# Sparse-attention outputs by tokens from unscaled weights, with a column of ones for the sums

## The chip, the cores and the metric

The kernel runs on one core of a Trainium2 chip. The metric is the device time of one launch, in microseconds (us). TensorE is PE in the profile (its weight loads are PEld), VectorE is DVE, ScalarE is ACT, GpSimd is POOL, and SyncE, which issues the large DMAs, is SP.

## The reference, cut to what matters

A two-layer transformer over 256 tokens of width 1024, in fp32. The first layer's mixer has 16 query heads of 64, in two groups that share keys and values, and three branches: compressed, selected and window. For each head the branch outputs are weighted by gates and added:

```python
s = jnp.where(mask, s, -inf)             # one branch, one head
e = jnp.exp(s - max(s))
p = e / sum(e)                            # masked_softmax
o = einsum('bthgk,bkgd->bthgd', p, v)     # p @ v, v: 64 wide, shared by 8 heads
out = g0 * o_cmp + g1 * o_slc + g2 * o_win
y = (out * sigmoid(z)) @ w_out
```

With 256 tokens the selected and the window branch both come down to causal attention here, each with its own keys and values, and both are computed in one loop.

## The kernel before, in words

`Net.run` calls the first layer's attention (`_nsa`), a dilated attention, feed-forward layers, a hybrid mixer and norms in turn. Weights come from DRAM in blocks of 128 x 2048 on SP's queue into the buffers `raw`; ACT makes a rounded high part (`hi`, L216), DVE the rest (`lo`, L219), and PE multiplies with both (banks `g`). Beside that, the modulation vectors of the layers are made on DVE from further blocks, two `scalar_tensor_tensor` of 128 x 1024 a block (L371). `self.step` and `self.fill` put such blocks, and matmuls of a projection that are ready early, between the steps of the attention. A scheduler at build time then sets a fixed order for each engine, and each engine runs its own in order.

PSUM has 8 banks: three with the tag `g`, two `s` (scores), two `t` (transposes), and **one** `o` (outputs). A bank is given to its next use when all readers of the last one are done.

The loop is `for j in range(8)`, one pair of heads (`hh` 0 and 1) per turn, numbered from pair 0; `g = j // 4` is the key group. For each head and each half of the query tokens (`q` = 1, tokens 128 to 255 against 256 keys; `q` = 0, tokens 0 to 127 against 128 keys) PE makes scores of both branches in a bank `s`, DVE takes their maxima (`mxs`, L925), ACT makes exponentials `p1` or `p0` (L927) and with `accum_out` their sums (`dens`). DVE inverts the sums (L929) and multiplies by the gates `gt` (L930); ACT scales `p1` (L934), DVE `p0` (L936). Three 128 x 128 transposes on PE (L213) bring each branch's weights into a bank `t` with the keys on the partitions, and a copy (L942, by ACT or DVE) puts them into one of six buffers (`kcat`, `kcp`, `pt0` to `pt2`, which hold 384 columns each).

The outputs come channels first. The values `vtok` (keys on the partitions, 64 channels) are the stationary operand, the weights of all 256 or the last 128 tokens are streamed, and the two heads write to the two halves of the partitions of one bank `o`, which also takes the compressed branch (`vb` stationary, `pct` streamed):

```python
ob = self.bank("o")
self.mm(ob[:, :256], vb[:, g, j % 4], pct[:, g], True, False)
...
va = vtok[:, k, br * 128 + g * 64:br * 128 + g * 64 + 64]
self.mm(ob[HALF[hh], 128 * k:256], va, pts[br, hh][:, 256 * k:256 + 128 * k], False, ...)
...
nc.scalar.copy(oT[:, j], ob[:, :256])    # L950
```

`oT` is then multiplied by the gate of `z` (L957), split into two parts, and goes into the output projection. L206 is the line of every matmul and L213 that of every transpose; an fp32 matmul appears as two passes.

Of the kernel before, what the change touches and what calls it, by code (L numbers as in the profile page):

```python
# [11 lines left out]
AF = mybir.ActivationFunctionType  # L12
ALU = mybir.AluOpType
# [5 lines left out]
HALF = slice(0, 64), slice(64, 128)  # L19
# [80 lines left out]
SC = ((0, 1), (1, 1))  # L100
# [57 lines left out]
class Net:  # L158
# [581 lines left out]
    def _nsa(self, xT):  # L740
        nc, A = self.nc, self.A
# [48 lines left out]
        i = nc.vector.tensor_tensor(self.og[:, :, 1], self.vec("final_g"), self.vec("final_g"), op=ALU.mult)  # L790
        self.tc.add_manual_dep(i.ins, self.applied.ins.name, NOSYNC, reason="norm first")
        nc.vector.tensor_scalar(self.og[:, :, 1], self.og[:, :, 1], EPS, None, op0=ALU.add)
        vtok = self.w([128, 512], tag="vtok", bufs=1).rearrange("p (q n) -> p q n", q=2)
        gt = self.w([128, 2, 16, 3], tag="gt", bufs=1)

        def ev_v(banks):
            for q in range(2):
                nc.vector.tensor_copy(vtok[:, q, :], banks[q][:, 0:256])
                nc.scalar.activation(gt[:, q].rearrange("p h r -> p (h r)"), banks[q][:, 256:304], AF.Tanh, scale=0.5)
            nc.vector.tensor_scalar(gt, gt, 1.0, None, op0=ALU.add)  # L800

        self.gemm(W, [(1408, 128), (1664, 128), (2816, 48)], act, ev_v, "B")
        zs = v8(self.b8())

# [13 lines left out]
        for vi, n in enumerate("kv"):  # L818
            ke = self.w([128, 16, 2, 16], tag="ke", bufs=1)
# [14 lines left out]
            t = self.t(self.sp, [32, 256], tag="hidt", bufs=1)  # L834
# [3 lines left out]
            b = self.bank("t")  # L838
# [7 lines left out]
        b = self.bank("t")  # L846
# [7 lines left out]
        vb = self.w([128, 2, 4, 128], tag="vb", bufs=1)  # L854
        bmv = self.C["bmv"].rearrange("p (j c) -> p j c", j=4)
        for g in range(2):
            b = self.bank("t")
# [19 lines left out]
        pc = self.w([128, 2, 16, 16], tag="pc", bufs=1)  # L877
        mx = self.w([128, 2, 16], tag="mx", bufs=1)
# [13 lines left out]
        pct = self.w([128, 2, 256], tag="pct", bufs=1)  # L892
        b = self.bank("t")
# [3 lines left out]
        nc.scalar.copy(pct.rearrange("p g t -> p (g t)"), b)  # L897

        kc, kp = self.w([128, 1024], tag="kcat", bufs=1), self.w([128, 512], tag="kcp", bufs=1)
        slots = [kc[:, :384], kc[:, 512:896], kp[:, :384]] + [self.t(self.sp, [128, 384], tag=f"pt{i}", bufs=1) for i in range(3)]  # L900
        self.rate = RN[1]
        oh, ol = (v8(self.b8(F32R)), v8(self.b8(F32R))) if OD[0] != (0, 1) or OD[1] != (0, 1) else (None, None)
        o32 = v8(self.b8()) if OD[0] or OD[1] else None
        oT = v8(self.b8())
        for j in range(8):
            g = j // 4
            self.fill(FN[6 + j])
            self.step(AN[6 + j])
            ob = self.bank("o")
            self.mm(ob[:, :256], vb[:, g, j % 4], pct[:, g], True, False)  # L910
            pts = {}
            for hh in range(2):
                h = 2 * j + hh
                p1 = self.t(self.sp, [128, 2, 256], tag="p1", bufs=2)
                p0 = self.t(self.sp, [128, 2, 128], tag="p0", bufs=2)
                mx = self.t(self.sp, [128, 2, 2], tag="mxs", bufs=2)
                den = self.t(self.sp, [128, 2, 2], tag="dens", bufs=2)
                for q in (1, 0):
                    p, nk = (p1, 256) if q else (p0, 128)
                    sb = self.bank("s")  # L920
                    sv = sb[:, :2 * nk].rearrange("p (b t) -> p b t", b=2)
                    for i, kx in enumerate((kh, kl)):
                        self.mm(sv, qs[g][:, j % 4, hh, q * 128:(q + 1) * 128], kx[:, g, :, :nk], i == 0, False)
                    self.mm(sv[:, :, nk - 128:], self.ibf, self.M["tri"][:, None, :].to_broadcast([128, 2, 128]), False, True)
                    nc.vector.tensor_reduce(mx[:, q], sv, axis=AX.X, op=ALU.max, negate=True)  # L925
                    for br in range(2):
                        nc.scalar.activation(p[:, br], sv[:, br], AF.Exp, bias=mx[:, q, br:br + 1],  # L927
                                             accum_out=den[:, q, br:br + 1])
                nc.vector.reciprocal(den, den)  # L929
                nc.vector.tensor_tensor(den, den, gt[:, :, h, 1:3], op=ALU.mult)  # L930
                for br in range(2):
                    for q, p in ((1, p1), (0, p0)):
                        if (br, q) in SC:
                            nc.scalar.activation(p[:, br], p[:, br], AF.Copy, scale=den[:, q, br:br + 1])  # L934
                        else:
                            nc.vector.tensor_scalar(p[:, br], p[:, br], den[:, q, br:br + 1], None, op0=ALU.mult)  # L936
                    tb = self.bank("t")
                    self.tr(tb[:, 0:128], p0[:, br, 0:128])
                    self.tr(tb[:, 128:256], p1[:, br, 0:128])
                    self.tr(tb[:, 256:384], p1[:, br, 128:256])  # L940
                    pt = slots[(4 * j + 2 * hh + br) % 6]
                    (nc.scalar.copy if (br, hh) in NPT else nc.vector.tensor_copy)(pt, tb[:, :384])  # L942
                    pts[br, hh] = pt

            for br in range(2):
                for k in range(2):
                    for hh in range(2):
                        va = vtok[:, k, br * 128 + g * 64:br * 128 + g * 64 + 64]
                        self.mm(ob[HALF[hh], 128 * k:256], va, pts[br, hh][:, 256 * k:256 + 128 * k], False, k == 1 and br == 1)
            nc.scalar.copy(oT[:, j], ob[:, :256])  # L950
        self.fill(99)
        for j in range(8):
            if o32 is None:
                t = self.w([128, 256], tag="xr", bufs=4)
            else:
                t = o32[:, j]
# [710 lines left out]
```

## Time and profile before

| | us |
|---|---|
| median of 3 runs (lowest, highest) | 1115.93 (1111.5, 1120.14) |
| the profiled execution | 1116.25 |
| its span in the trace | 1114.4 |
| PE busy in the span | 1059.9 |
| DVE busy | 859.6 |
| ACT busy | 615.9 |

The span runs from the first to the last instruction in the trace; the execution's own time is 1.85 us longer. The busy times are of the span. The mean granted clock of TensorE was 0.987 of full speed.

### The profile page before, as it was taken

The numbers are of one execution on the slowest core, as the hardware profiler recorded it, in microseconds if no ns is written. First come the engines' busy times: TensorE is split into PE (matmuls) and PEld (weight loads), VectorE is DVE, ScalarE is ACT, GpSimd is POOL, SyncE is SP. The second block draws the span as 40 slices with busy tenths as digits, with TensorE's granted clock in tenths as the row PEclk, the third lists the DMA queues.
The fourth block names the chain that finished last, engine by engine and source line by source line (L and its number), as shares of the span: only waits on it lengthen the run. The fifth ranks groups of instructions, "written<-read, shape, count | busy, mean of one in ns | idle before, by whom it ended". The sixth has DMA issues, their size and how long they took to land.

```text
span 1114.4 us, 20234 instructions
## 1 busy us (share of the span) xinstructions
PE 1059.9 (95%) x8145; PEld 990.3 (89%) x8145; DVE 859.6 (77%) x1571; ACT 615.9 (55%) x1190; POOL 64.3 (6%) x70
## 2 busy tenths in 40 slices
PE   5989999989999999999999899989999999999997
PEld 4958867877889899999989789989999999999997
DVE  7995987899999998888698789468866767555543
ACT  3482776788665544544378257525644556444442
POOL 0020000122000000000000030001000000000000
PEclk9898999999999999999999899999999999999998
DMA  8865466466868577887743433263436445554551
GB/s 332 336 223 189 155 224 232 174 242 226 310 238 296 177 291 302 299 300 282 288 153 128 142 114 114 83 187 114 149 121 246 169 158 181 189 190 170 173 186 39
DMA packets 33423, 226.34 MB, mean 203 GB/s; under 512 B 3681, under 2 KB 3937, under 8 KB 7346
## 3 DMA queue, kind: packets, MB, share of 16 engines
q1 hardware_dynamic: 32914, 224.20, 55.7%
q8 instruction: 64, 1.05, 0.4%
q10 hardware_dynamic: 288, 0.52, 0.1%
q0 software_dynamic: 128, 0.33, 0.1%
q14 instruction: 29, 0.24, 0.1%
HBM read 223.73 MB, written 1.31 MB: 202 GB/s over the span
## 4 chain that ended last, share of the span: by engine, by line
issue 35%; PE 21%; DVE 6%; DMA 2%; ACT 2%; POOL 1%; SPq 0%; POOLq 0%; DVEq 0%; ACTq 0%
PE g L206 14%; PE s L206 5%; DMA b<-dr 2%; DVE lo L219 1%; PE t L206 1%; PE o L206 1%; DVE w L1221 1%; PE t L213 1%; POOL rrq L1282 0%; DVE xt L1371 0%; ACT hi L216 0%; DVE b L1450 0%; DVE b L1459 0%; DVE xs L1372 0%; DVE d L1443 0%
## 5 line engine op out<-in xcount | busy, mean ns | idle before, releaser
L206 PE MATMUL g<-b,hi 128*128 128x256 f32 (+2 forms) x3696 | 688.0, 286 | 9.8 <-ACT b L586 8.1
L206 PEld LDWEIGHTS g<-b,hi 128*128 128x128 f32 (+1 forms) x3696 | 578.2, 191 | 16.2 <-ACT b L586 9.8
L206 PE MATMUL g<-b,lo 128*128 128x256 f32 (+2 forms) x1848 | 518.6, 285 | 8.6 <-DVE lo L219 8.6
L216 ACT CAST hi<-raw 128x1024 fp32r<-128x1024 f32 (+2 forms) x302 | 280.0, 953 | 222.1 <-PE g L206 117.2
L219 DVE TENSOR_TENSOR lo<-raw,hi 128x1024 fp32r<-128x1024 f32 (+2 forms) x302 | 329.8, 1114 | 90.2 <-ACT hi L216 89.8
L206 PEld LDWEIGHTS g<-b,lo 128*128 128x128 f32 (+1 forms) x1848 | 347.9, 190 | 12.0 <-DVE lo L219 10.4
L371 DVE SCALAR_TENSOR_TENSOR raw<-raw,scrow 128x1024 f32<-128x1024 f32 x120 | 146.0, 1238 | 4.9 <-DMA raw<-in_ws_dram 4.8
L206 PE MATMUL s<-b,hi 128*128 128x256 f32 (+1 forms) x288 | 62.8, 284 | 2.2 <-ACT w L546 2.2
L206 PE MATMUL s<-b,b 128*128 128x128 f32 (+2 forms) x224 | 49.8, 344 | 3.6 <-DVE b L682 1.9
L206 PE MATMUL g<-b,raw 128*128 128x256 f32 x208 | 51.3, 381 | 0.0
L206 PEld LDWEIGHTS s<-b,hi 128*128 128x128 f32 x288 | 48.4, 189 | 2.4 <-ACT w L546 2.4
L1221 DVE SCALAR_TENSOR_TENSOR w<-pad,u,w 128x256 f32<-128x256 f32 x96 | 41.7, 481 | 2.5 <-ACT w L1216 2.4
L206 PEld LDWEIGHTS g<-b,raw 128*128 128x128 f32 x208 | 37.1, 190 | 4.7 <-ACT w L546 0.2
L206 PEld LDWEIGHTS s<-b,b 128*128 128x128 f32 x224 | 30.1, 191 | 11.4 <-issue 4.5
L206 PE MATMUL s<-b,lo 128*128 128x256 f32 (+1 forms) x144 | 39.7, 283 | 0.0
L206 PE MATMUL t<-b,hi 128*128 128x256 f32 x160 | 37.5, 281 | 0.0
L927 ACT ACTIVATE p<-s,mxs 128x256 f32<-128x256 f32 (+1 forms) x64 | 26.5, 420 | 13.8 <-DVE dens L930 6.2
L1132 DVE TENSOR_TENSOR w<-w,g 128x512 f32<-128x512 f32 (+1 forms) x21 | 14.2, 675 | 23.7 <-PE g L206 23.7
L488 POOL TENSOR_TENSOR rcol<-rcol,u 128x2 f32<-128x2 f32 x5 | 3.5, 703 | 487.3 <-ACT rcol L487 487.3
L206 PE MATMUL g<-hi,b 128*128 128x512 f32 (+1 forms) x96 | 28.3, 371 | 2.4 <-ACT hi L216 2.3
L1130 ACT ACTIVATE w<-g 128x512 f32<-128x512 f32 (+1 forms) x21 | 12.3, 586 | 32.0 <-PE g L206 32.0
L206 PEld LDWEIGHTS t<-b,hi 128*128 128x128 f32 x160 | 28.5, 188 | 0.0
(329 smaller groups left out, 1314.2 us busy)
## 6 DMA issues: line engine op xcount, KB each, us to landing
raw<-in_ws_dram SPq DMA_DIRECT2D x202, 1024.0 KB, 4.8
b<-dr SPq DMA_DIRECT2D x8, 512.0 KB
raw<-in_ws_dram SPq DMA_DIRECT2D x4, 512.0 KB, 3.7
raw<-in_ws_dram SPq DMA_DIRECT2D x2, 608.0 KB, 3.8
b<-in_xT_dram SPq DMA_DIRECT2D x1, 1024.0 KB
u<-in_consts_dram SPq DMA_DIRECT2D x2, 384.0 KB
u<-in_consts_dram SPq DMA_DIRECT2D x1, 527.0 KB
u<-in_consts_dram SPq DMA_DIRECT2D x2, 256.0 KB, 5.5
```

What stands on the lines that cost most here:

```text
L206: i = self.nc.tensor.matmul(out, lhsT=lhsT, rhs=rhs, start=start, stop=stop, skip_group_check=True)
L213: self.nc.tensor.transpose(out, in_, self.ident[:k, :k])
L216: i = self.nc.scalar.copy(hi, src)
L219: self.nc.vector.tensor_tensor(lo, src, hi, op=ALU.subtract)
L371: nc.vector.scalar_tensor_tensor(r, r, 1.0, sc, op0=ALU.mult, op1=ALU.mult, accum_out=mod[:, n:n + 1])
L488: nc.gpsimd.tensor_tensor(r, r, self.mhalf[:, 0:2], op=ALU.pow)
L927: nc.scalar.activation(p[:, br], sv[:, br], AF.Exp, bias=mx[:, q, br:br + 1], accum_out=den[:, q, br:br + 1])
L1130: nc.scalar.activation(t, gb, AF.Tanh, scale=0.5)
L1132: nc.vector.tensor_tensor(t, t, ub, op=ALU.mult)
L1221: nc.vector.scalar_tensor_tensor(dst, fl(pad[:, o:o + 256]), taps[i], dst, op0=ALU.mult, op1=ALU.add)
```

## The change

`vtok` becomes `vone`, which holds 65 columns per half, branch and group: 64 of values and one of ones, set once by POOL. `accum_out`, the inversion per head and the scaling of `p1` and `p0` leave the loop, so the transposes and the copies take unscaled exponentials. For each pair and each half `q` (1, then 0) one bank `o` takes the compressed branch (now `pct` stationary, 128 columns of `vb` streamed) and, beside it, 65 columns for each head and branch (the weights stationary, `vone` streamed), so the tokens lie on the partitions and column 64 holds the sums. DVE inverts these (L947), multiplies by the gates (L948), scales the four 64-column pieces (`obs`, in the buffer `ke`; L950), adds the compressed branch (L951) and adds the two branches (L952) into `on`, in the buffer `pc`. After both halves, two transposes bring `on` into a bank `t`, and ACT copies it to `oT`. Lines below the loop move: L957 is L963 there.

```diff
@@ -790,12 +790,13 @@
         i = nc.vector.tensor_tensor(self.og[:, :, 1], self.vec("final_g"), self.vec("final_g"), op=ALU.mult)
         self.tc.add_manual_dep(i.ins, self.applied.ins.name, NOSYNC, reason="norm first")
         nc.vector.tensor_scalar(self.og[:, :, 1], self.og[:, :, 1], EPS, None, op0=ALU.add)
-        vtok = self.w([128, 512], tag="vtok", bufs=1).rearrange("p (q n) -> p q n", q=2)
+        vone = self.w([128, 2, 4, 65], tag="vtok", bufs=1)
+        nc.gpsimd.memset(vone[:, :, :, 64:65], 1.0)
         gt = self.w([128, 2, 16, 3], tag="gt", bufs=1)
 
         def ev_v(banks):
             for q in range(2):
-                nc.vector.tensor_copy(vtok[:, q, :], banks[q][:, 0:256])
+                nc.vector.tensor_copy(vone[:, q, :, :64], banks[q][:, 0:256].rearrange("p (v e) -> p v e", v=4))
                 nc.scalar.activation(gt[:, q].rearrange("p h r -> p (h r)"), banks[q][:, 256:304], AF.Tanh, scale=0.5)
             nc.vector.tensor_scalar(gt, gt, 1.0, None, op0=ALU.add)
 
@@ -897,6 +898,8 @@
         nc.scalar.copy(pct.rearrange("p g t -> p (g t)"), b)
 
         kc, kp = self.w([128, 1024], tag="kcat", bufs=1), self.w([128, 512], tag="kcp", bufs=1)
+        obs = self.w([128, 2, 2, 2, 64], tag="ke", bufs=1)
+        ons = self.w([128, 2, 2, 128], tag="pc", bufs=1)
         slots = [kc[:, :384], kc[:, 512:896], kp[:, :384]] + [self.t(self.sp, [128, 384], tag=f"pt{i}", bufs=1) for i in range(3)]
         self.rate = RN[1]
         oh, ol = (v8(self.b8(F32R)), v8(self.b8(F32R))) if OD[0] != (0, 1) or OD[1] != (0, 1) else (None, None)
@@ -906,15 +909,11 @@
             g = j // 4
             self.fill(FN[6 + j])
             self.step(AN[6 + j])
-            ob = self.bank("o")
-            self.mm(ob[:, :256], vb[:, g, j % 4], pct[:, g], True, False)
             pts = {}
             for hh in range(2):
-                h = 2 * j + hh
                 p1 = self.t(self.sp, [128, 2, 256], tag="p1", bufs=2)
                 p0 = self.t(self.sp, [128, 2, 128], tag="p0", bufs=2)
                 mx = self.t(self.sp, [128, 2, 2], tag="mxs", bufs=2)
-                den = self.t(self.sp, [128, 2, 2], tag="dens", bufs=2)
                 for q in (1, 0):
                     p, nk = (p1, 256) if q else (p0, 128)
                     sb = self.bank("s")
@@ -924,16 +923,8 @@
                     self.mm(sv[:, :, nk - 128:], self.ibf, self.M["tri"][:, None, :].to_broadcast([128, 2, 128]), False, True)
                     nc.vector.tensor_reduce(mx[:, q], sv, axis=AX.X, op=ALU.max, negate=True)
                     for br in range(2):
-                        nc.scalar.activation(p[:, br], sv[:, br], AF.Exp, bias=mx[:, q, br:br + 1],
-                                             accum_out=den[:, q, br:br + 1])
-                nc.vector.reciprocal(den, den)
-                nc.vector.tensor_tensor(den, den, gt[:, :, h, 1:3], op=ALU.mult)
+                        nc.scalar.activation(p[:, br], sv[:, br], AF.Exp, bias=mx[:, q, br:br + 1])
                 for br in range(2):
-                    for q, p in ((1, p1), (0, p0)):
-                        if (br, q) in SC:
-                            nc.scalar.activation(p[:, br], p[:, br], AF.Copy, scale=den[:, q, br:br + 1])
-                        else:
-                            nc.vector.tensor_scalar(p[:, br], p[:, br], den[:, q, br:br + 1], None, op0=ALU.mult)
                     tb = self.bank("t")
                     self.tr(tb[:, 0:128], p0[:, br, 0:128])
                     self.tr(tb[:, 128:256], p1[:, br, 0:128])
@@ -941,13 +932,28 @@
                     pt = slots[(4 * j + 2 * hh + br) % 6]
                     (nc.scalar.copy if (br, hh) in NPT else nc.vector.tensor_copy)(pt, tb[:, :384])
                     pts[br, hh] = pt
-
-            for br in range(2):
-                for k in range(2):
-                    for hh in range(2):
-                        va = vtok[:, k, br * 128 + g * 64:br * 128 + g * 64 + 64]
-                        self.mm(ob[HALF[hh], 128 * k:256], va, pts[br, hh][:, 256 * k:256 + 128 * k], False, k == 1 and br == 1)
-            nc.scalar.copy(oT[:, j], ob[:, :256])
+            on = ons[:, j % 2]
+            for q in (1, 0):
+                ob = self.bank("o")
+                ov = ob[:, :260].rearrange("p (h b e) -> p h b e", h=2, b=2)
+                cb = ob[:, 260:388].rearrange("p (h e) -> p h e", h=2)
+                f = self.mm(ob[:, 260:388], pct[:, g, q * 128:(q + 1) * 128], vb[:, g, j % 4])
+                for hh in range(2):
+                    for br in range(2):
+                        for k in range(q + 1):
+                            c0 = 128 * (q + k)
+                            self.mm(ov[:, hh, br], pts[br, hh][:, c0:c0 + 128], vone[:, k, br * 2 + g], False, k == q, f)
+                r = self.t(self.sp, [128, 2, 2], tag="dens", bufs=2)
+                nc.vector.reciprocal(r, ov[:, :, :, 64])
+                nc.vector.tensor_tensor(r, r, gt[:, q, 2 * j:2 * j + 2, 1:3], op=ALU.mult)
+                t = obs[:, q]
+                nc.vector.tensor_tensor(t, ov[:, :, :, :64], r[:, :, :, None].to_broadcast([128, 2, 2, 64]), op=ALU.mult)
+                nc.vector.tensor_tensor(t[:, :, 0], t[:, :, 0], cb, op=ALU.add)
+                nc.vector.tensor_tensor(on[:, q].rearrange("p (h e) -> p h e", h=2), t[:, :, 0], t[:, :, 1], op=ALU.add)
+            tb = self.bank("t")
+            for q in range(2):
+                self.tr(tb[:, q * 128:(q + 1) * 128], on[:, q])
+            nc.scalar.copy(oT[:, j], tb[:, :256])
         self.fill(99)
         for j in range(8):
             if o32 is None:
```

The order on the engines changes with it. On PE between pairs, before (bank `o_207` is pair 1's output, `o_224` pair 2's, `s_237` and `s_238` are scores):

```order
L206 MATMUL o_207_1187<-pt2_168_1024,vtok_101_673 64x256 [waits Activation_49]
L206 MATMUL o_207_1187<-pt0_166_1022,vtok_101_673 64x128
L206 MATMUL o_207_1187<-pt2_168_1024,vtok_101_673 64x128
L206 MATMUL s_237_1306<-b8_23_127,b8_26_130 128x512 [waits PE_49,Activation_49]
L206 MATMUL s_237_1306<-b8_23_127,b8_26_130 128x512
L206 LDWEIGHTS u150_150_913
L206 MATMUL s_237_1306<-u149_149_911,u150_150_913 128x2x128
L206 MATMUL s_238_1313<-b8_23_127,b8_26_130 128x256 [waits Activation_49]
L206 MATMUL s_238_1313<-b8_23_127,b8_26_130 128x256
L206 MATMUL o_224_1266<-pct_162_1013,vb_141_892 128x256 [waits Activation_49]
```

And the changed order there (`o_210` is pair 1's half `q` = 0, `o_227` pair 2's half `q` = 1, `t_212` the transposes of `on`, which is named `pc_167`; `t_218` those of pair 2's weights):

```order
L206 MATMUL o_210_1188<-vb_141_893,pct_162_1014 128x128 [waits DVE_49]
L206 MATMUL o_210_1188<-vtok_101_673,pt1_169_1026 128x65
L206 MATMUL o_210_1188<-vtok_101_673,pt2_170_1027 128x65
L206 MATMUL o_210_1188<-vtok_101_673,kcat_164_1021 128x65 x2
L206 MATMUL o_227_1258<-vb_141_893,pct_162_1014 128x128 [waits DVE_49,PE_49]
L213 MATMUL t_212_1200<-u7_7_89,pc_167_1024 128x128 [waits DVE_49]
L213 MATMUL t_212_1200<-u7_7_89,pc_167_1024 128x128
L213 MATMUL t_218_1221<-u7_7_89,p0_214_1205 128x128
L213 MATMUL t_218_1221<-u7_7_89,p1_213_1204 128x128 x2
```

The scores now stand ahead of pair 1's last half, and the compressed matmul of pair 2 and the transposes of `on` follow that half with no other matmul between.

On DVE at that place, before (the step from one head's sums to its scaled weights in pair 2; L371 and L219 are work of other layers or the projection):

```order
L929 RECIPROCAL dens_228_1271<-dens_228_1271 128x4 [waits Activation_49]
L925 TENSOR_REDUCE mxs_235_1304<-s_237_1306 128x2 [waits PE_49]
L930 TENSOR_TENSOR dens_228_1271<-dens_228_1271,gt_102_674 128x4 [waits DVE_49]
L668 SCALAR_TENSOR_TENSOR b8_116_754<-w5_323_1786,g_310_1662 128x512 [waits Activation_49]
L936 TENSOR_SCALAR p0_226_1269<-p0_226_1269,dens_228_1271 128x128 [waits DVE_49]
L936 TENSOR_SCALAR p0_226_1269<-p0_226_1269,dens_228_1271 128x128
L925 TENSOR_REDUCE mxs_235_1304<-s_238_1313 128x2 [waits PE_49]
L957 SCALAR_TENSOR_TENSOR b8_171_1027<-b8_172_1028,b8_116_754 128x256
L942 COPY kcat_164_1020<-t_231_1290 128x384 [waits PE_49]
```

And the changed order (the five steps on pair 1's half `q` = 0, in `o_210`):

```order
L947 RECIPROCAL dens_211_1194<-o_210_1188 128x4 [waits PE_49]
L371 SCALAR_TENSOR_TENSOR raw_353_1960,u15_15_109<-raw_353_1960,scrow_9_94 128x1024
L948 TENSOR_TENSOR dens_211_1194<-dens_211_1194,gt_102_675 128x4 [waits DVE_49]
L371 SCALAR_TENSOR_TENSOR raw_357_1973,u15_15_109<-raw_357_1973,scrow_9_94 128x1024 [waits DMAHW7_49]
L950 TENSOR_TENSOR ke_166_1023<-o_210_1188,dens_211_1194 128x256 [waits DVE_49]
L371 SCALAR_TENSOR_TENSOR raw_357_1973,u15_15_109<-raw_357_1973,scrow_9_94 128x1024
L951 TENSOR_TENSOR ke_166_1023<-ke_166_1023,o_210_1188 128x2x64 [waits DVE_49]
L952 TENSOR_TENSOR pc_167_1024<-ke_166_1023 128x128 [waits DVE_49]
L963 SCALAR_TENSOR_TENSOR b8_173_1030<-b8_174_1031,b8_116_755 128x256 [waits Activation_49]
```

Three L371 stand between the five steps, of which the first and third read the bank, as does the fourth.

On PE at the last pair, before (`o_292` is pair 7's output; `t_350` belongs to the output projection):

```order
L206 MATMUL o_292_1582<-kcat_164_1020,vtok_101_673 64x256 [waits Activation_49]
L206 MATMUL o_292_1582<-pt1_167_1023,vtok_101_673 64x128
L206 MATMUL o_292_1582<-kcat_164_1020,vtok_101_673 64x128
L206 MATMUL o_292_1582<-pt2_168_1024,vtok_101_673 64x256
L206 MATMUL o_292_1582<-kcat_164_1020,vtok_101_673 64x256 [waits Activation_49]
L206 MATMUL o_292_1582<-pt2_168_1024,vtok_101_673 64x128
L206 MATMUL o_292_1582<-kcat_164_1020,vtok_101_673 64x128
L206 MATMUL t_350_1956<-b8_171_1027,raw_351_1957 128x256 [waits PE_49]
L206 MATMUL t_350_1956<-b8_171_1027,raw_351_1957 128x256 x2
```

And the changed order (`o_324` is pair 7's half `q` = 0, `t_326` the transposes of its `on`, `t_368` and `g_344` are of the output projection and the `z` projection):

```order
L206 MATMUL o_324_1704<-vb_141_893,pct_162_1014 128x128 [waits DVE_49,PE_49]
L206 MATMUL o_324_1704<-vtok_101_673,pt1_169_1026 128x65
L206 MATMUL o_324_1704<-vtok_101_673,pt2_170_1027 128x65
L206 MATMUL o_324_1704<-vtok_101_673,kcat_164_1021 128x65 x2
L213 MATMUL t_326_1716<-u7_7_89,pc_167_1024 128x128 [waits DVE_49]
L213 MATMUL t_326_1716<-u7_7_89,pc_167_1024 128x128
L206 MATMUL t_368_2015<-b8_173_1030,raw_369_2016 128x256 x3
L206 MATMUL g_344_1878<-b8_171_1028,hi_351_1908 128x256 [waits Activation_49]
L206 MATMUL g_344_1878<-b8_171_1028,lo_352_1909 128x256
```

The transposes now stand between the last output matmul and the projection.

## Rows read from the trace of the kernel before

**Rows 1.** The page's part 1: busy us, share of the span, instructions.

```profile
PE 1059.9 (95%) x8145; PEld 990.3 (89%) x8145; DVE 859.6 (77%) x1571; ACT 615.9 (55%) x1190; POOL 64.3 (6%) x70
```

**Rows 2.** Windows, the loop and what follows: us; PE, PEld, DVE, ACT, POOL; clock; DMA; GB/s.

```profile
121.00:189.00 68.00, 66.12 (x422) 47.58 (x422) 58.28 (x153) 53.13 (x182) 0.00 (x0) 1.00 0.57 204
190.00:1100.00 910.00, 884.45 (x7015) 848.72 (x7015) 699.10 (x1224) 495.75 (x886) 50.52 (x54) 0.99 0.55 198
```

**Rows 3.** Waits of PE from 121 to 189 us: total us, times, longest.

```profile
PE t L213 <- DVE p L936: 1.2, 2, 0.7
PE o L206 <- DVE kcat L942: 0.4, 1, 0.4
```

**Rows 4.** Timeline of PE at one pair: start, us, operation.

```profile
141.30 0.43 PE L206 MATMUL o<-pt,vtok 128*64 128x256 f32 x1
141.30 0.43 PE L206 MATMUL o<-kcp,vtok 128*64 128x128 f32 x2
141.56 1.25 PE L206 MATMUL o<-pt,vtok 128*64 128x256 f32 x11
142.74 0.73 PE L206 MATMUL s<-b,b 128*128 128x512 f32 x2
...
146.95 0.65 PE L206 MATMUL o<-kcat,vtok 128*64 128x256 f32 x2
147.53 0.28 PE L206 MATMUL s<-u,u 128*128 128x256 bf16 x1
...
148.02 1.89 PE L206 MATMUL g<-b,raw 128*128 128x256 f32 x8
149.75 0.82 PE L213 MATMUL t<-u,p 128*128 128x128 f32 x6
150.40 0.38 PE L206 MATMUL g<-b,raw 128*128 128x256 f32 x1
```

**Rows 5.** Timeline of PE, fp32 passes with 128 and 32 streamed columns elsewhere.

```profile
99.50 1.30 PE L206 MATMUL o<-kb,b 128*128 128x32 f32 x10 [0.49 <-DVE kb L853]
100.64 0.69 PE L206 MATMUL t<-w,hx 128*128 128x128 f32 x4
...
716.92 5.40 PE L206 MATMUL s<-b,b 128*128 128x128 f32 x46
722.08 0.37 PE L206 MATMUL g<-b,hi 128*128 128x256 f32 x1
```

**Rows 6.** DVE by line and form, 120 to 190 us: busy us, mean ns | idle before.

```profile
L371 DVE SCALAR_TENSOR_TENSOR raw<-raw,scrow 128x1024 f32<-128x1024 f32 x21 | 25.2, 1218 | 1.4 <-DMA raw<-in_ws_dram 1.4
L925 DVE TENSOR_REDUCE mxs<-s 128x2 f32<-128x512 f32 x13 | 8.8, 679 | 2.6 <-PE s L206 2.4
L936 DVE TENSOR_SCALAR p<-p,dens 128x128 f32<-128x128 f32 x28 | 6.6, 280 | 0.0
L219 DVE TENSOR_TENSOR lo<-raw,hi 128x1024 fp32r<-128x1024 f32 x5 | 5.9, 1222 | 2.1 <-ACT hi L216 2.1
L925 DVE TENSOR_REDUCE mxs<-s 128x2 f32<-128x256 f32 x13 | 5.5, 421 | 2.2 <-PE s L206 2.2
...
L929 DVE RECIPROCAL dens<-dens 128x4 f32<-128x4 f32 x14 | 2.4, 174 | 1.2 <-ACT p L927 1.1
L930 DVE TENSOR_TENSOR dens<-dens,gt 128x4 f32<-128x4 f32 x14 | 2.2, 155 | 0.0
```

**Rows 7.** The same view of DVE, 105 to 121 us: a 128 x 256 read from PSUM.

```profile
L880 DVE TENSOR_TENSOR pc<-o,u 128x256 f32<-128x256 f32 x2 | 0.7, 416 | 0.0
```

**Rows 8.** The same view of ACT, 120 to 190 us.

```profile
L934 ACT ACTIVATE p<-p,dens 128x256 f32<-128x256 f32 x28 | 12.6, 500 | 1.6 <-DVE dens L930 1.6
L927 ACT ACTIVATION_READ_ACCUMULATOR p<-s,mxs 128x1 f32 x56 | 11.4, 203 | 0.0
...
L950 ACT COPY b<-o 128x256 f32<-128x256 f32 x8 | 3.0, 372 | 4.0 <-PE o L206 3.8
L216 ACT CAST b<-b 128x256 fp32r<-128x256 f32 x7 | 2.9, 411 | 0.0
```

## The prediction

> **What bounds the kernel now.** I read the busy times of the page first, then the same by stages, then the waits of the stage that is changed, and last its instructions. PE is busy 95% of the span [rows 1]; in the loop over the pairs, 121 to 189 us, it is busy 66.12 of 68 us, and in the 910 us behind it 884.45 [rows 2]. The reader is to see two things there: the loop has 1.9 us of PE idle time at most to win back, and what it loses can't be made up later, since PE has no slack there either. The waits agree: in the loop PE waits 1.2 us for scaled weights (L936) and 0.4 us for a copy [rows 3]. DVE is busy 58.28 and ACT 53.13 of the 68 us [rows 2]. So work taken off ACT or DVE gains little by itself; PE's own instructions count in full, and so does each wait that is put into its order. The granted clock is 1.00 in the loop [rows 2], the upper of the two levels, and I leave it there.
>
> **PE's instructions.** Per pair, before: the 16 passes of the output matmuls stood in one block of 14, which took 142.74 - 141.30 = 1.44 us, and a further two, which took 147.53 - 146.95 = 0.58 [rows 4]. A pass with 256 streamed columns and its neighbour on the other half of the array start together there (two rows begin at 141.30), which is why 14 take so little. The compressed matmul is two passes of 256 columns. The nearest row for one is the 0.43 of a single 256-column pass, which is a duration and not a spacing; I take 0.43 for the pair of them, by the spacing 0.22 that the block shows (1.44 us for seven side-by-side couples, 0.21 each). Sum 1.44 + 0.58 + 0.43 = 2.45 us.
> After: 12 output matmuls (for q = 1 two heads, two branches, two key blocks; for q = 0 half of that) make 24 passes, two compressed ones make 4, each with 128 stationary columns and 65 or 128 streamed. No row has 65 columns. With 128, 46 passes take 722.08 - 716.92 = 5.16 us, 0.112 each; with 32, ten take 100.64 - 99.50 = 1.14, 0.114 each [rows 5]. 65 lies between and both give the same, so 28 x 0.112 = 3.14. Two transposes of `on` at (150.40 - 149.75) / 6 = 0.108 [rows 4] add 0.22. Sum 3.36, so 0.91 more a pair and **+7.3 us** for eight.
> The Trainium skill, "TensorE: Matmul & The Clock Gate", section "Back-to-back issue gap", gives about 81 ns for each matmul in a stream of weight loads and matmuls with 128 columns. By that, 28 passes and two transposes would take 2.49 us, PE's work would be unchanged, and the sum below would be 7 us lower. The 46 passes at 0.112 are such a stream and do not agree, so the measurement decides.
>
> **Entering a wait.** The two passes that stood alone took 0.58 where two neighbours take about 0.43 [rows 4]: 0.15 for being started apart, behind a wait. In PE's order of the loop 124 rows waited before and 96 do now, since unscaled weights come from ACT alone and not half from DVE. 28 x 0.15 = 4.2 us. That is an estimate from one place; its ends are 0 (a wait that is already met costs nothing) and 4.2. I take **-4.2 us**, because PE's 422 recorded rows have small gaps of this kind all along the loop.
>
> **DVE and ACT.** The change takes off DVE 32 L936 (28 lie in the window) at 0.28 and 16 each of L929 and L930 at 0.17 and 0.16 [rows 6]: 9.0 + 5.3 = 14.2 us. It adds per pair and half 0.17 + 0.16 for the small ones, 0.42 for the 128 x 256 product out of PSUM (L880 is such a one [rows 7]), and 0.28 each for the two additions of 128 columns, by L936, the nearest in size: 1.31 us, x16 = 21.0. DVE gains 6.7 us of work and would be busy 65 us in a loop of about 70. ACT loses 64 reads of the accumulator at 0.20 and 32 L934 at 0.50 [rows 8], 29 us; it isn't the bound, so I count it at nothing, and it is why the waits in front of the weights' transposes (1.2 us [rows 3]) should go. The copies to `oT` stay as they are (0.37 [rows 8]). The ones by POOL are set once in the setup; POOL is busy 6% [rows 1]. No DMA is added or removed.
>
> **New waits.** This is the largest term. There is one bank `o`, now used twice a pair, and its reader was one ACT copy; now it is three of the five DVE steps. PE can't write the next half before L951 is done, nor transpose `on` before L952. Behind the waiting instruction stands everything else on PE. What it costs depends on what the fixed order puts beside it, and the order of the changed kernel shows four bad places.
> Pair 1 to 2 (shown in the section on the change): the steps hold three L371, 1.22 each [rows 6], and PE has nothing between the last output matmul and the compressed one: 0.17 + 1.22 + 0.16 + 1.22 + 0.42 + 1.22 + 0.28 = **4.7 us**.
> Pair 2 to 3: two maxima (0.68 and 0.42 [rows 6]) and one L371 stand in the steps up to L951, 0.17 + 0.68 + 0.16 + 0.42 + 0.42 + 1.22 + 0.28 = 3.35; PE has 0.5 us of scores beside it (from the row at 147.53 to that at 148.02 [rows 4]), so 2.85. A second L371 stands before L952: 1.22 + 0.28 less the 0.22 of the compressed matmul. Together **4.1 us**.
> Pair 5 to 6: a wide L219 (1.22 [rows 6]) takes the place of the first L371, and PE has 1.6 us of scores and projection, one matmul of which waits for that L219: 0.3 + 1.7, and another L219 before L952, 1.3. **3.3 us**.
> Last pair (shown): PE waits for five steps, 1.31, and after two transposes for ACT's copy, the gate's product (about 0.42), and the rounding (0.41 [rows 8]), 1.2 us of which some 0.5 lies beside three matmuls; before, the projection had six there. **2.0 us**.
> The sum is **14.1 us**. The other places hold no long DVE work, or PE has matmuls beside: I put them at 0, and for the upper end at 3.6, half a microsecond for the second bank use of the pairs not named. Another unknown is the bank `t`: five sets of transposes in a row now go through two banks, each behind ACT's copy; ends 0 and 5 us, and I take 0, since ACT has 29 us less to do.
>
> **Sum.** 1116.25 + 7.3 - 4.2 + 14.1 = 1133.5 us, against the profiled execution's own time, which is 0.3 us above the median of the runs. I say **1134**.
>
> **Rivals.** *Only PE's work counts.* The long DVE work is run while PE still makes scores, because DVE reaches those rows earlier than I walk it: with 29 us less on ACT the chain from scores to transposes is shorter, so DVE is ahead of PE. For it: the L371 wait only for a block that has landed, and 1.4 us of idle time was put down to that [rows 6]. Against it: the L371 stand behind L947, which waits for PE, so in order they can't run before. Then 1116.25 + 7.3 - 4.2 + 0 to 5 of waits = 1119 to 1124, within 1%.
> *Faster: ACT's relief.* The place is the front of each head's transposes. If PE's 66.12 us of busy time holds waits that the trace counts as work (a matmul that stands behind the one before it counts as busy until its end), the shorter chain from the maxima to the copies takes them out. At 0.5 us for each of 32 sets, half of L934's 0.50 with the read of 0.20 that now leave the chain [rows 8], that is 16 us; with +7.3 and 5 us of new waits, 1112. It decides for a faster kernel once more than 12 us come out; for one faster by over 1% more than 18.5 must come out and no new wait be left: the whole 0.70 a set, 22 us, gives 1101. Against it: of 68 us, PE waits 1.6 [rows 2, 3].
> *All waits as walked, and more.* With 3.6 us of small ones, 5 of the banks `t`, and half of the 4.2 us for waits not saved: 1133.5 + 3.6 + 5 + 2.1 = 1144, the upper end.
>
> **How the numbers follow.** The forecast, 1127 to 1144, has a chance of 0.62; the first rival 0.24; the faster one 0.14, of which 0.07 beyond 1%. About 1% is what a measurement of this kernel can tell from no change, 11 us here, so the line to slower lies at 1127. Slower is the forecast's 0.62 and 0.02 for the first rival with all of the small waits; within 1% are the rest of that rival, 0.22, and half of the faster one, 0.07; faster is its other half, 0.07. The range runs from 1117, which leaves out the faster rival for the most part, to 1144.
>
> **What would show it.** In the changed trace: about 28 passes on `o` a pair at 0.112 us, PE busy some 7 us more in the loop; waits of PE on `o` and on the transposes for DVE's L951 and L952 of about 14 us, the largest near the end of pair 1, beside L371; ACT some 29 us less busy; DVE some 7 more; the stages behind the loop unchanged in length. I am wrong if PE's idle time in the loop stays near 2 us, if the passes with 65 columns are spaced well under 0.112, or if the stages behind the loop change by more than the loop does.

## The result and the profile after

The changed kernel took 1154.43 us (median of 4 runs, 1153.53 to 1162.03) against 1114.97 (4 runs, 1111.5 to 1120.14): a ratio of 1.0339, 95% interval 1.0296 to 1.0382. Slower was forecast, by 18 us; it is 39, outside the range. The page of the profiled execution, to be read beside [rows 1]:

```profile
span 1151.7 us, 20352 instructions
PE 1081.9 (94%) x8241; PEld 1017.0 (88%) x8241; DVE 866.8 (75%) x1587; ACT 597.3 (52%) x1094; POOL 64.2 (6%) x71
```

The span grew by 37.3 us. PE is idle 1151.7 - 1081.9 = 69.8 us of it, and was idle 54.5; and it is busy 22 us longer. The windows of the loop show why a busy PE took longer, which [rows 2] do not (columns as there; the eighth is the granted clock). The first row is the loop from the second head's first maximum (L924) to the start of the last copy to `oT`; the others are stretches in it:

```profile
109.70:223.60 113.90, 95.44 (x606) 81.93 (x605) 80.54 (x201) 42.68 (x109) 0.00 (x0) 0.89 0.44 157
...
133.80:140.60 6.80, 6.80 (x30) 6.12 (x29) 3.07 (x8) 2.31 (x7) 0.00 (x0) 0.50 0.56 211
140.60:147.50 6.90, 3.43 (x23) 2.81 (x21) 5.96 (x14) 0.68 (x3) 0.00 (x0) 0.99 0.16 31
147.50:154.30 6.80, 5.89 (x26) 5.41 (x26) 4.66 (x11) 3.33 (x9) 0.00 (x0) 0.50 0.69 277
...
164.50:174.80 10.30, 9.49 (x39) 8.07 (x40) 5.28 (x14) 4.04 (x11) 0.00 (x0) 0.50 0.58 205
...
222.50:226.00 3.50, 3.15 (x9) 2.61 (x10) 1.14 (x3) 0.78 (x2) 0.29 (x1) 0.51 0.35 101
```

In four stretches, 27.4 us together, the clock is at its lower level, 1.2 GHz, and PE is busy in 25.3 us of them; in the loop before it never fell [rows 2]. Each begins in a wait of PE or right behind one. The same loop before, from the same maximum to the same copy:

```profile
112.10:189.00 76.90, 74.67 (x486) 55.02 (x485) 67.05 (x175) 59.23 (x198) 0.00 (x0) 1.00 0.55 194
```

These are the waits of PE in the loop (us in total, times, longest), beside [rows 3]:

```profile
PE o L206 <- DVE ke L951: 9.6, 6, 4.4
PE t L213 <- DVE pc L952: 3.4, 4, 1.6
PE t L213 <- DVE pc L890: 1.7, 1, 1.7
PE s L206 <- ACT p L926: 0.8, 1, 0.8
PE t L213 <- ACT b L956: 0.7, 1, 0.7
PE t L213 <- ACT pt L933: 0.6, 1, 0.6
PE t L213 <- ACT kcat L933: 0.6, 1, 0.6
```

The 1.7 us on L890 belong to the compressed branch, ahead of the first outputs; `no_chain` and `b_noscale` below have this wait too, so it does not come from the new DVE steps. The longest wait, in the timeline of all engines (start, us, engine, operation, idle before): the end of pair 1.

```profile
143.42 0.61 PE L206 MATMUL o<-vtok,kcat 128*128 128x65 f32 x4
...
144.06 0.18 DVE L947 RECIPROCAL dens<-o 128x4 f32<-128x4 f32 x1 [0.21 <-PE o L206]
144.16 1.19 DVE L371 SCALAR_TENSOR_TENSOR raw<-raw,scrow 128x1024 f32<-128x1024 f32 x1
...
145.28 0.16 DVE L948 TENSOR_TENSOR dens<-dens,gt 128x4 f32<-128x4 f32 x1
145.36 1.22 DVE L371 SCALAR_TENSOR_TENSOR raw<-raw,scrow 128x1024 f32<-128x1024 f32 x1
...
146.50 0.42 DVE L950 TENSOR_TENSOR ke<-o,dens 128x256 f32<-128x256 f32 x1
146.84 1.22 DVE L371 SCALAR_TENSOR_TENSOR raw<-raw,scrow 128x1024 f32<-128x1024 f32 x1
...
147.98 0.28 DVE L951 TENSOR_TENSOR ke<-ke,o 128x128 f32<-128x128 f32 x1
...
148.41 0.77 PE L206 MATMUL o<-vb,pct 128*128 128x128 f32 x2 [4.38 <-DVE ke L951]
```

Four steps of 0.16 to 0.42 us take from 144.06 to 148.26, since three L371 stand between them, and PE has nothing else in its order. The two passes behind the wait take 0.77 us where the same two took 0.38 to 0.46 elsewhere in the loop: the clock has gone down by then.

So the growth can be split. Lost clock, (1 - 0.987) x 1114.4 before and (1 - 0.975) x 1151.7 after, is 14.5 and 28.8 us; what is left of PE's busy time, its work at full clock, is 1045.4 and 1053.1. Idle +15.3, clock +14.3, work +7.7: 37.3 us. (The clock has three digits, so each lost time is good to 0.6 us, and slow stretches in which PE was idle are counted both as idle and as lost clock.) The two rows of the loop give a check without that double count: PE's idle time there went from 2.2 to 18.5 us; of the 20.8 us that it was busy longer, half of the 25.3 us that it was busy at the lower clock, 12.7 us, is an estimate of what the clock took, and 8.1 is added work. So the loop holds 37.0 of the 37.3 us, and waits and clock are 29 of them.

### The profile page after: what moved, and what is told of

Its sections match the earlier page's. It is cut to its first block, busy times and chain, and to the rows that moved or that the text cites. A ratio compares the mean times of both kernels' runs of the same rounds, so it can differ in the third digit from the quotient of the medians.

```text
span 1151.7 us, 20352 instructions
## 1 busy us (share of the span) xinstructions
PE 1081.9 (94%) x8241; PEld 1017.0 (88%) x8241; DVE 866.8 (75%) x1587; ACT 597.3 (52%) x1094; POOL 64.2 (6%) x71
## 4 chain that ended last, share of the span: by engine, by line
PE 39%; issue 36%; DVE 15%; ACT 6%; DMA 3%; POOL 1%; SPq 0%; DVEq 0%; POOLq 0%; ACTq 0%
PE g L206 22%; PE s L206 7%; PE o L206 6%; DVE raw L371 3%; DVE lo L219 3%; PE t L213 2%; PE t L206 2%; DMA b<-dr 2%; ACT w L677 1%; ACT hi L216 1%; DVE w L1227 1%; DVE mxs L924 1%; ACT b L585 1%; DVE w L678 1%; ACT b L586 1%
## 5 line engine op out<-in xcount | busy, mean ns | idle before, releaser
L219 DVE TENSOR_TENSOR lo<-raw,hi 128x1024 fp32r<-128x1024 f32 (+2 forms) x302 | 328.7, 1110 | 90.6 <-ACT hi L216 90.1
L371 DVE SCALAR_TENSOR_TENSOR raw<-raw,scrow 128x1024 f32<-128x1024 f32 x120 | 146.1, 1237 | 4.3 <-DMA raw<-in_ws_dram 4.2
L926 ACT ACTIVATE p<-s,mxs 128x256 f32<-128x256 f32 (+1 forms) x64 | 23.3, 426 | 28.1 <-DVE mxs L924 19.2
L1136 ACT ACTIVATE w<-g 128x512 f32<-128x512 f32 (+1 forms) x21 | 12.3, 588 | 33.0 <-PE g L206 33.0
```

The lines of the kernel that those rows point to most:

```text
L219: self.nc.vector.tensor_tensor(lo, src, hi, op=ALU.subtract)
L371: nc.vector.scalar_tensor_tensor(r, r, 1.0, sc, op0=ALU.mult, op1=ALU.mult, accum_out=mod[:, n:n + 1])
L1136: nc.scalar.activation(t, gb, AF.Tanh, scale=0.5)
```

## The experiments

The theory: PE's own work costs some 7 us; the five DVE steps, stretched by long DVE work, hold the one bank `o` and the transposes, and PE waits; and the waits bring the clock down, which costs as much again. The rivals: the new passes themselves are dear, and the waits only where it shows; or the clock falls because of the kind of passes. All runs in one table: ratio to the kernel before with its interval, and from each profile the span, PE's idle time (span less busy), the lost clock as above, and PE's work without it. The profile columns are of one execution each. In the sessions of these runs the kernel before had medians of 1119.5 to 1121.2 us, some 5 us more than in the result, so expectations in us are best read against the ratios.

| kernel | ratio (95%) | span | idle | lost clock | work |
|---|---|---|---|---|---|
| before | 1 | 1114.4 | 54.5 | 14.5 | 1045.4 |
| changed | 1.0339 (1.0296, 1.0382) | 1151.7 | 69.8 | 28.8 | 1053.1 |
| act_copy | 1.0126 (1.0083, 1.0169) | 1132.9 | 61.3 | 18.1 | 1053.5 |
| late_only | 1.0119 (1.0059, 1.0180) | 1131.2 | 59.8 | 20.4 | 1051.0 |
| act_copy_late | 1.0055 (1.0030, 1.0079) | 1124.9 | 56.5 | 15.7 | 1052.7 |
| no_chain | 1.0021 (0.9990, 1.0052) | 1114.1 | 50.5 | 13.4 | 1050.2 |
| scaled_form | 1.0015 (0.9980, 1.0050) | 1120.3 | 54.5 | 13.4 | 1052.4 |
| b_noscale | 0.9946 (0.9926, 0.9966) | 1111.8 | 51.2 | 14.5 | 1046.1 |
| dve_copy | 1.0212 (1.0172, 1.0251) | 1142.0 | 68.1 | 19.4 | 1054.5 |
| short_371 | 1.0125 (1.0080, 1.0170) | 1129.1 | 60.2 | 14.7 | 1054.2 |
| b_short_371 | 0.9940 (0.9908, 0.9971) | 1112.7 | 53.9 | 13.4 | 1045.4 |
| dummy_fill | 1.0305 (1.0267, 1.0344) | 1153.2 | 63.1 | 24.2 | 1065.9 |
| pool_hold | 1.0298 (1.0250, 1.0347) | 1155.6 | 72.1 | 35.8 | 1047.7 |
| pool_hold_fill | 1.0338 (1.0259, 1.0417) | 1148.0 | 63.8 | 17.2 | 1067.0 |

`act_copy_late` and `pool_hold` have the same PE instructions, and their work differs by 5.0 us in the last column, so a few us there say little. The scheduler also set a new fixed order for each of these kernels. Line numbers shift a little from kernel to kernel: the last of the five DVE steps is L952 in the changed kernel, L953 in `short_371` and L955 in `act_copy` and `dve_copy`.

**The form without its chain.** `no_chain`:

```diff
-                (the five DVE steps, L946 to L952)
+                nc.scalar.copy(on[:, q], ob[:, :128])
```

> The changed kernel without the five DVE steps: ACT copies 128 columns of bank o straight to the buffer that is transposed. It leaves out the division by the sums, the gates and the addition of the branches, so the output is not the reference's; PE's instructions are all there. Waits and clock: PE's added work of 7 us, less some waits: 1118 to 1126. Passes: 1140 to 1155.

The ratio is 1.0021, with the same 8241 recorded matmuls as the changed kernel. The rival of dear passes falls. Two more runs part the form (outputs by tokens) from the relief (no sums and no scaling of weights): `scaled_form` is `no_chain` with the sums and the scaling of the kernel before put back, and `b_noscale` is the kernel before with these taken out:

```diff
-                nc.vector.reciprocal(den, den)
-                nc.vector.tensor_tensor(den, den, gt[:, :, h, 1:3], op=ALU.mult)
...
-                        if (br, q) in SC:
...
```

> The kernel before with the outputs made by tokens, from weights that are scaled as before, and with ACT copying 128 columns of bank o straight to the buffer that is transposed back: the new form's PE work with the old ACT and DVE work. It leaves out part of the compressed branch and the addition of the branches, so the output is not the reference's. By the prediction's sum, PE's added work of 7.3 us and no saved waits: ratio to the kernel before 1.005 to 1.008. If the added work is less than counted, as in a stream that is not bound by weight loads: 0.999 to 1.003, as with the unscaled weights and no chain (1.0021).

> The kernel before without the sums, their inversion and the scaling of the weights (so the output is not the reference's); outputs are made channels first, as before. It is ACT's and DVE's relief alone, 29 us of ACT and 14 of DVE. By the prediction's term for waits that are entered, 4.2 us faster: ratio 0.996. By the rival of ACT's relief, 16 us: ratio 0.985. If neither matters, since PE is the bound: 1.000.

The relief alone gives 0.54% (6 us), near the 4.2 of the term for waits and far from the 16 of the rival of ACT's relief; PE's work is the same there (1046.1) and idle time is 3.3 us less. The form alone is 1.0015, interval 0.998 to 1.005, which is 1.7 us, at most 5.6, and inside the second range expected, of less work than counted; by the work column it is 7.0 us. The two don't agree well, and what the form costs is known only as some 2 to 8 us.

**Freeing the bank, and moving the transposes.** `act_copy` (`ocs` are two buffers of 512 columns):

```diff
+                nc.scalar.copy(ocs[q][:, :388], ob[:, :388])
+                ov = ocs[q][:, :260].rearrange("p (h b e) -> p h b e", h=2, b=2)
+                cb = ocs[q][:, 260:388].rearrange("p (h e) -> p h e", h=2)
```

`late_only` puts the transposes of a pair one pair later (`back` holds the four lines that are taken out below); `act_copy_late` does both:

```diff
+            if j:
+                back(j - 1)
             on = ons[:, j % 2]
...
-            tb = self.bank("t")
-            for q in range(2):
-                self.tr(tb[:, q * 128:(q + 1) * 128], on[:, q])
-            nc.scalar.copy(oT[:, j], tb[:, :256])
+        back(7)
```

> The changed kernel, but ACT copies the 388 used columns of each bank o, and the five DVE steps read the copy, so that the bank is free after one ACT copy and not after L951. Waits and clock (PE waits some 17 us for DVE in the loop, and the granted clock falls to the lower level behind each long wait, some 13 us more): the waits on the bank (9.6 us) go, those of the transposes stay in part, the clock stays up for the most part: 1125 to 1135. Passes (the new form costs PE itself 30 us, the waits are only where it shows): 1150 to 1155. Clock by kind of work (short passes bring the clock down by themselves): half-speed stretches stay, 1140 to 1150.

> The changed kernel with the transposes of a pair's outputs one pair later, and nothing else: bank o is still held until DVE has done L951. If the bank is the main cause: most of the 9.6 us of waits on it stay, with the clock behind them, ratio 1.02 to 1.03. If the transposes at the end of a pair are: ratio 1.005 to 1.012, as with ACT's copy.

> As the one with ACT's copy, and the two transposes of a pair's outputs are written one pair later in the program, so that nothing on PE waits for the five DVE steps at once. Waits and clock: what is left is PE's added work of 7 us and little else, 1118 to 1126, with the clock of the loop near 1.00. Passes: 1145 to 1155. Clock by kind of work: half-speed stretches stay, 1135 to 1145.

Each alone takes back some 2.1% of the 3.4, both together 2.8%. In `act_copy` no wait on the bank is left, and 2.8 us on the transposes of `on`. That the bank is the main cause, the first case expected of `late_only`, does not hold: with the bank still held by DVE its waits fell from 9.6 to 2.6 us,

```profile
PE o L206 <- DVE ke L958: 2.6, 2, 1.6
```

and the order then has transposes, scores and projection between a pair's outputs and the next use of the bank. It takes the two together, the held bank and the transposes right behind it, to leave PE with nothing. In `act_copy_late` the loop runs at the upper clock, with the same passes:

```profile
121.00:195.40 74.40, 70.51 (x526) 62.30 (x527) 63.75 (x175) 44.81 (x116) 0.00 (x0) 1.00 0.48 171
```

It is still 0.55% slower than before. That this is the form's work is not shown, and no version of this form was measurably faster than the kernel before.

**The long work between the steps.** `dve_copy` is `act_copy` with `nc.vector.tensor_copy` in place of ACT's copy. `short_371` cuts 18 of the 24 L371 in the loop to 64 columns; `b_short_371` does so in the kernel before:

```diff
-                    r = raw[:, k * 1024:(k + 1) * 1024]
+                    m = 64 if (a block of the loop) else 1024
+                    r = raw[:, k * 1024:k * 1024 + m]
```

> As the one in which ACT copies the 388 columns of each bank, but DVE makes the copy, so DVE stands between PE and the free bank, as in the changed kernel, with one step and not with four, and does 16 copies more (some 9 us). If the long DVE work between the steps holds the bank: waits on the bank of 1 us or less at a time, ratio 1.012 to 1.02. If any wait for DVE's queue does it: ratio 1.025 to 1.035, as the changed kernel.

> The changed kernel, but the 18 L371 of the nine blocks that the order puts into the loop work on 64 of their 1024 columns (the blocks are fetched as before; the sums that they make are left incomplete, so the output is not the reference's). The five DVE steps, the one bank and the place of the transposes are as in the changed kernel, and PE has nothing more to do beside. If the long DVE work between the steps makes the waits: the wait at the end of pair 1 falls from 4.4 us to about 1, the waits to half or less, few half-speed stretches: ratio 1.008 to 1.018. If the bank and the late transposes are enough by themselves: ratio 1.025 to 1.034.

> The kernel before with the same 18 L371 cut to 64 columns, as a control: what 20 us less of DVE work is worth where DVE isn't waited for. DVE not the bound: ratio 0.995 to 1.002. If DVE's work had a hidden part in PE's time: 0.985 to 0.995.

With short L371 the changed kernel is at 1.0125, and its loop (121 to 200.6 us) runs at a clock of 1.00. The waits of its PE in the loop:

```profile
PE t L213 <- DVE pc L953: 2.0, 2, 1.6
PE t L213 <- DVE pc L891: 1.7, 1, 1.7
PE o L206 <- DVE raw L372: 1.4, 1, 1.4
PE o L206 <- DVE ke L952: 0.8, 2, 0.5
```

The wait at the end of pair 1 is 1.4 us, and was 4.4. Not all of that is the shorter DVE work, since the order moved as well: scores now stand behind pair 1's last outputs, about 1.0 us, where the changed kernel had nothing:

```profile
137.48 0.61 PE L206 MATMUL o<-vtok,kcat 128*128 128x65 f32 x4
137.90 0.70 PE L206 MATMUL s<-b,b 128*128 128x512 f32 x2
...
140.46 0.46 PE L206 MATMUL o<-vb,pct 128*128 128x128 f32 x2 [1.37 <-DVE raw L372]
```

The control gained 0.6%, more than expected, so of the 2.1% that the short L371 gave back, some 0.6% is, by the control, what less DVE work gives anyway; the other 1.5% is the long work's place between the steps together with the moved order, which this run does not part. In `dve_copy` the bank is free after one step (0.5 us of waits on it), but the wait went on to the transposes, which stand behind the same steps:

```profile
PE t L213 <- DVE pc L955: 11.9, 5, 3.8
```

Its timeline at the end of a pair:

```profile
151.36 0.42 DVE L953 TENSOR_TENSOR ke<-ke,dens 128x256 f32<-128x256 f32 x1
151.69 1.22 DVE L371 SCALAR_TENSOR_TENSOR raw<-raw,scrow 128x1024 f32<-128x1024 f32 x1
...
153.04 1.22 DVE L371 SCALAR_TENSOR_TENSOR raw<-raw,scrow 128x1024 f32<-128x1024 f32 x1
...
154.19 0.28 DVE L955 TENSOR_TENSOR pc<-ke 128x128 f32<-128x128 f32 x1
...
154.53 0.54 PE L213 MATMUL t<-u,pc 128*128 128x128 f32 x2 [3.40 <-DVE pc L955]
```

Its 1.0212 is just above the range that I gave to the long work, and its interval touches both ranges; it is the waits that tell the two apart, not the time.

**The clock.** `dummy_fill` puts dummy matmuls where PE waits:

```diff
+                if q == 0:
+                    for _ in range(ND[j]):       # ND = (6, 18, 12, 0, 0, 6, 0, 6)
+                        f = self.mm(ob[:, 388:512], self.ident[:, :128], self.ident[:, :124], False, True, f)
```

> The changed kernel with 48 dummy matmuls of 124 columns (96 passes, 10.8 us at 0.112) into unused columns of bank o behind the last output matmul of pairs 0, 1, 2, 5 and 7, where PE waits for DVE; nothing reads them. Waits and clock: PE is busy in the waits, the granted clock stays at the upper level there, and the kernel is faster although PE does more: 1142 to 1149. Passes, or a clock that falls with short passes: the dummies are more of the same, the time is the changed kernel's or longer: 1154 to 1165.

It was not faster by what I expected: 1.0305, between the two cases, with an interval that includes the changed kernel's ratio. Against the changed kernel PE does 12.8 us more work, is idle 6.7 less and loses 4.6 less of the clock. At the end of pair 1, 36 dummy passes and some scores stand for the 4.4 us, but waits of 1.6 and 0.8 us follow them, and behind these the one stretch of this loop at the lower level (columns of the last row as above):

```profile
146.74 4.23 PE L207 MATMUL o<-u 128*128 128x124 f32 x36
...
153.01 0.46 PE L207 MATMUL o<-vb,pct 128*128 128x128 f32 x2 [1.57 <-DVE ke L955]
154.27 0.44 PE L214 MATMUL t<-u,pc 128*128 128x128 f32 x2 [0.80 <-DVE pc L956]
...
155.90:166.20 10.30, 9.88 (x37) 8.71 (x37) 6.03 (x15) 3.99 (x12) 0.00 (x0) 0.50 0.57 205
```

So with 96 more short passes the slow time in the loop went from 27.4 to 10.3 us, which speaks against a clock that falls with short passes. I had overlooked that a dummy in a shorter wait costs its time.

`pool_hold` makes PE wait without more work for PE, DVE or ACT, on `act_copy_late`; `pool_hold_fill` adds dummies ahead of these waits (views of the operands left out):

```diff
+                    if br and hh:
+                        for _ in range(3):
+                            nc.gpsimd.tensor_tensor(pt, pt, ones, op=ALU.mult)
...
+                        if q and hh and br:
+                            for _ in range(9):
+                                self.mm(ob[:, 388:512], self.ident[:, :128], self.ident[:, :124], False, True, f)
```

> The version with ACT's copy and late transposes, plus three multiplications by one on POOL (128 x 384, some 1.2 us each) on the last of each pair's transposed weights before PE may use them: PE's, DVE's and ACT's work is the same, and PE waits, if the matmuls beside are used up, 2 to 4 us in a pair. Waits bring the clock down: half-speed stretches come back in the loop behind the waits, and the time grows by more than the waits: with 15 us of waits, 20 to 28 us. Clock independent of waits: no half-speed stretch, and the time grows by the waits alone.

> The version with the multiplications on POOL, and nine dummy matmuls of 124 columns a pair (144 passes in all, 16 us at 0.112) into unused columns of bank o, right ahead of the matmul that waits for POOL; nothing reads them. The end of each wait is set by POOL, so the dummies lie in time that PE waited anyway. Idle time brings the clock down: the half-speed stretches of the loop (34 us, PE busy in nearly all) go or shrink, and the kernel is 10 to 17 us faster though PE does 16 us more: ratio to the kernel before 1.013 to 1.021. The clock falls for another reason: half-speed stretches stay, ratio 1.03 or more.

The waits of PE on POOL in `pool_hold`, and two of its windows:

```profile
PE o L206 <- POOL pt L941: 10.6, 5, 2.5
PE o L206 <- POOL kcat L941: 7.5, 3, 2.6
```

```profile
138.10:144.90 6.80, 6.72 (x31) 6.72 (x32) 3.10 (x10) 4.03 (x10) 0.03 (x1) 0.50 0.19 77
...
223.50:230.20 6.70, 6.70 (x33) 6.70 (x33) 2.75 (x11) 1.27 (x3) 0.00 (x0) 0.50 0.38 152
```

With 18.1 us of waits on POOL the span is 30.7 us longer than that of `act_copy_late` (27 us by the two ratios): idle time grew by 15.6 us and lost clock by 20.1. Six stretches of the loop, 33.9 us with PE busy in 31.7, are at the lower level, and none was without the waits. So waits bring it down with the same passes. With the dummies two such stretches are left in the loop, 3.4 us each, though PE still waits 12.3 us for POOL:

```profile
121.00:168.90 47.90, 40.21 (x317) 35.87 (x316) 39.25 (x82) 22.10 (x55) 16.71 (x12) 1.00 0.46 168
168.90:172.30 3.40, 3.40 (x16) 3.11 (x16) 1.65 (x5) 1.85 (x5) 0.00 (x0) 0.51 0.03 7
```

The time did not fall (1.0338, with a wide interval; the mean clock of its four runs was 0.985, 0.978, 0.983 and 0.976, where `pool_hold` had 0.969 to 0.975). The windows are of the fastest of the four; in the two slowest the clock is little above `pool_hold`'s best. What the clock gave back, the 144 dummy passes took: PE's idle time is only 8.3 us less than in `pool_hold`, for some 19 us more work. For the time it is a miss; for what brings the clock down it agrees.

The Trainium skill, "TensorE: Matmul & The Clock Gate", section "What's actually happening", says that the array has two clock states, chosen by how busy TensorE has been. The traces here agree: 1.00 and 0.50 are the only two that the stretches show.

## Why the prediction was wrong

**The bound** was read rightly: PE had next to no slack in the loop, and the waits put into its order counted.

**The step that failed** is a sentence of the first part: "The granted clock is 1.00 in the loop [rows 2], the upper of the two levels, and I leave it there." It was 1.00 in a loop where PE waited for DVE 1.6 us in all [rows 3]. The prediction put 14 us of waits in its order and kept the clock; in the changed kernel 27.4 us of the loop ran at half clock, and lost clock in the whole kernel grew by 14.3 us. That this follows from the waits is what `pool_hold` shows. With these 14.3 us added to the sum, and the term of 4.2 us not taken off, it comes to 1116.25 + 7.3 + 14.1 + 14.3 = 1152, against 1154; since 14.3 is measured and not forecast, that only says that nothing large is missing. Of the signs of being wrong that the prediction names, none looks at the clock.

**PE's instructions**, +7.3: the work column gives +7.7 and the loop's two rows 8.1, but the time of `scaled_form` only 1.7, at most 5.6, so the size of this term stays open. The passes with 65 columns are 0.10 to 0.11 us apart at the upper clock, near the 0.112 assumed. The 81 ns of the Trainium skill, "TensorE: Matmul & The Clock Gate", section "Back-to-back issue gap", do not fit that spacing.

**Entering a wait**, -4.2: no such gain is left in the changed kernel, where new waits drown it. `b_noscale` gives 6 us for the relief, which is near in size; that it comes from waits that are no longer entered is not shown, and `b_short_371` gained as much with those waits in place.

**New waits**, +14.1. The four places, walked and measured: pair 1 to 2, 4.7 and 4.38; pair 2 to 3, 4.1 and 2.64 + 0.80; pair 5 to 6, 3.3 and 1.12 + 0.79; last pair, 2.0 and 1.58. That is 11.3 for 14.1, and small ones that I had put at 0, with the 1.7 us on L890, make up for it: idle time grew by 15.3. Walking both orders row by row with the trace's durations held to about a fifth.

**ACT**, counted at nothing in the sum: its busy time fell by 18.6 us (615.9 to 597.3) and not by 29. The prediction added up the lengths of rows, and these overlap in the trace: a read of the accumulator that starts at 141.88 us lasts 0.21, and the next activation starts at 141.97. DVE's 7.2 more (859.6 to 866.8) are the forecast 7.

**The rivals.** "Only PE's work counts" is what `no_chain` shows; it needs the chain away. "ACT's relief" gave 6 us and not 16. That all waits come and more, the upper end, had no clock in it either, so the range ended 10 us too low.

## What to carry to other kernels

Where PE is the bound, price a new wait twice: once for itself, and once for the half clock that can follow it; here 18 us of waits cost 27 to 31 (`pool_hold`). Before changing who empties a bank, read in the fixed order what stands between the reader's steps and what PE has beside them: small steps on DVE (0.16 to 0.42 us) took 4.2 us together because three long instructions were put in between. Let an engine with room copy the bank out in one step, and place whatever needs the result one turn later: that took 1.0339 to 1.0055 here, not below the kernel before.

## What was not expected of the hardware

Waits of 0.2 to 0.7 us that lie close together (0.21, 0.70 and 0.61 us between 130 and 133.5 us of the changed kernel) also had a stretch at the lower clock behind them, 6.8 us; while `pool_hold_fill` waited for POOL eight times, up to 2.5 us, and fell to it twice in the loop, and a wait of 2.5 us at the end of pair 2 in `dummy_fill` had no such stretch behind it. Which waits bring it down these runs don't settle. And the control `b_short_371` gained 0.6% from 18 shorter DVE instructions in a loop where PE waited for DVE 1.6 us in all [rows 3]; where that came from was not followed up.
